# Row-major attention in spaced turns, the GELU as one operation, and weight halves made by two DMAs

## The chip, the cores and the metric

The kernel runs on one core of a Trainium2 chip. The metric is the time of one execution on the device in microseconds (us): the median of three runs is 1231.18 us (1231.11 to 1231.23). The traces were taken by the hardware profiler in one more execution each.

## The reference, cut to what matters

An encoder of two layers over 512 tokens (a grid of 8 rows of 64) with 1024 channels. All arrays are float32.

```
for l in range(2):
    h = rmsnorm(x, g_mix[l]);  z = h @ w_in[l]            # 1024 -> 2560
    q, k, v, x_rec, gate = split(z, 512 each)
    att = neighbourhood_attention(q, k, v, rel_bias[l])   # 8 heads, each token sees 8 x 16 tokens
    xc = depthwise_conv(x_rec, 4 taps)
    rec = (rg_lru forward + rg_lru backward)(xc) * gelu(gate, approximate=True)
    x = x + concat(rmsnorm(att), rmsnorm(rec)) @ w_out[l]
    h = rmsnorm(x, g_ffn[l]);  u_act, u_lin = split(h @ w_up[l])        # 1024 -> 2 x 3072
    x = x + (gelu(conv3(u_act)) * u_lin) @ w_down[l]
return rmsnorm(x, g_final)
```

The approximate GELU is `0.5 z (1 + tanh(sqrt(2/pi) (z + 0.044715 z^3)))`.

## The kernel before

Channels lie on the 128 partitions and the 512 tokens along the free axis, so an activation is some tiles of 128x512. Each float32 product is made of three matmuls in the type float32r (`mm3`, lines 187 to 190): every operand is split into a rounded half `hi` and a remainder `lo`, and `hi*hi`, `hi*lo` and `lo*hi` are summed in PSUM.

**The weights** come in chunks of 128x1024 (eight blocks of 128x128), in the order in which they are used (`weight_plan`, line 49). `load_to` (line 152) starts a DMA on SyncE's queue into one of two `raw` tiles; `split_to` (line 162) lets ScalarE copy `raw` into `hi` (line 171, which rounds) and VectorE write `raw - hi` into `lo` (line 172). There are four `hi` and four `lo` tiles, used in turn, so a chunk's halves can't be written before the chunk that stands four places ahead of it has been used. `chunk` (line 176) hands out a chunk and asks for splits three chunks ahead and loads six chunks ahead. A chunk of `w_in` is one column of the projection: 24 matmuls of 512 tokens.

**The mixing stage** of a layer begins with the four recurrent columns (`xr`), then follows the list `MIX` (line 43), a hand-written order of steps: `q`, `k`, `v`, `g` are columns of the projection (`a` and `b` its halves), `c` a convolution, `t` the gates and scans of one recurrent tile (12 matmuls and much work on ScalarE and VectorE), `u` turns a value tile into tokens by channels, `S` makes the scores and the softmax of a pair of heads for half of the columns of the grid, `T` transposes the probabilities, `P` multiplies them with the values, `o` is a part of the output projection, `n` the statistics. A planner then orders the instructions of each engine by priority and by its own costs; `urgent()` raises the priority of what stands under it, and before the change `S` and `T` stand under it as a whole (lines 724 and 727), matmuls included.

**Attention** works on tokens in column-major order (eight rows of a grid column next to each other). `query_tile` (line 509) writes two tiles per pair of heads with zeros in the other head's half (GpSimd's memsets, line 517, and four VectorE products of 64x256, line 528); `key_tile` and `value_tile` write column-major too (lines 536 and 547); line 679 turns the attention's output back to row-major. `value_tokens` lets GpSimd copy four shifted pieces into the two `edge` tiles (line 564), which `P` reads.

**The GELU of the gate** (`gate_tile`, line 573) is a VectorE evacuation (578), a square (ScalarE, 580), three VectorE operations (581, 582, 584), a Tanh (ScalarE, 583) and a last product with `fb` (585).

After the mixing stage come `w_up` and `w_down` (the MLP), whose chunks are split in the same way.

Of the kernel before, what the change touches and what calls it, by code (L numbers as in the profile page):

```python
# [99 lines left out]
def encoder(ctx: ExitStack, tc: tile.TileContext, x_d, w_d, cols_d, bias_d, out_d):  # L100
# [13 lines left out]
    p_t = pool("p_t", 12)  # L114
# [30 lines left out]
    raws, halves = {}, {}  # L145
# [5 lines left out]

    def load_to(n):
        while state["load"] < min(n, len(plan)):
            i = state["load"]
            raws[i] = p_raw.tile([P, 1024], F32, tag="raw", name=f"raw{i}")
            for n, sl in enumerate(pieces(i)):
                nc.sync.dma_start(raws[i][:, sl], w_d[i][:, sl])
                if i == n == 0:
                    nc.sync.dma_start(x[0], x_d[0])
            state["load"] += 1  # L160

    def split_to(n):
# [94 lines left out]

    NL = 16
# [168 lines left out]
    def layer(l, xn):  # L427
# [81 lines left out]
        def query_tile(i):  # L509

            qk[i] = [big(p_h, "h", f"q{l}{i}{n}") for n in range(2)]

            def zones(other):
                return [by_head(t[64 * a:64 * a + 64])[:, :, a ^ other] for t in qk[i] for a in (0, 1)]

            for z in zones(1):
                nc.gpsimd.memset(z, 0.0)  # L517
            ps = psum(ps_mm, f"qps{l}{i}")
            yield from column_parts(ps, "w_in", l, i, xg, 4)
            with urgent():  # L520
                for n, z in enumerate(zones(0)):
                    rows = slice(64 * (n % 2), 64 * (n % 2) + 64)
                    cs = slice(32 * (n // 2), 32 * (n // 2) + 32)

                    def grid(ap):
                        return by_row(ap)[rows, :, cs].rearrange("p r (j c) -> p r j c", c=8)

                    nc.vector.tensor_tensor(out=z.rearrange("p j (c r) -> p r j c", r=ROWS), in0=grid(ps),  # L528
                                            in1=grid(rb), op=ALU.mult)

        def key_tile(i):
# [10 lines left out]
        def value_tile(i):  # L542
# [3 lines left out]
            with urgent():  # L546
                nc.vector.tensor_tensor(out=by_column(o), in0=by_row(ps), in1=by_row(rb), op=ALU.mult)
# [24 lines left out]

        def gate_tile(t):
            ps = psum(ps_mm, f"gate{l}{t}")
            yield from column_parts(ps, "w_in", l, 16 + t, xg, 4)
            z = big(p_t, "t", f"z{l}{t}")
            with urgent():
                nc.vector.tensor_tensor(out=z, in0=ps, in1=rb, op=ALU.mult)
            s = big(p_t, "t", f"zs{l}{t}")
            nc.scalar.activation(s, z, AF.Square)  # L580
            nc.vector.tensor_scalar(out=s, in0=s, scalar1=0.044715, scalar2=1.0, op0=ALU.mult, op1=ALU.add)
            nc.vector.tensor_tensor(out=s, in0=s, in1=z, op=ALU.mult)
            nc.scalar.activation(s, s, AF.Tanh, scale=math.sqrt(2.0 / math.pi))
            nc.vector.scalar_tensor_tensor(out=z, in0=s, scalar=1.0, in1=z, op0=ALU.add, op1=ALU.mult)
            nc.vector.scalar_tensor_tensor(out=fb[t], in0=fb[t], scalar=0.5, in1=z, op0=ALU.mult, op1=ALU.mult)
# [17 lines left out]
        def scores(h):  # L603
            blocks = range(4 * (h % 2), 4 * (h % 2) + 4)
            bt, qt, kt = bias[h // 2], qk[h // 2][h % 2], qk[4 + h // 2]
# [4 lines left out]
            for pair in (blocks[0:2], blocks[2:4]):  # L610
                ps = psum(ps_s, f"s{l}{h}{pair[0]}")
                o = 0
                for b in pair:
                    kc0, w, _ = BLOCKS[b]
                    nc.tensor.matmul(ps[:, o:o + ROWS * w], qt[:, b % 4 * P:(b % 4 + 1) * P],  # L615
                                     kt[:, ROWS * kc0:ROWS * (kc0 + w)], start=True, stop=True)
# [3 lines left out]
                for b in pair:  # L620
                    _, w, bo = BLOCKS[b]
                    nc.vector.tensor_tensor_reduce(out=pr[b][0], in0=pr[b][1], in1=bt[:, bo:bo + ROWS * w], scale=1.0,  # L622
                                                   scalar=-3e38, op0=ALU.add, op1=ALU.max,
                                                   accum_out=mx[:, b % 4:b % 4 + 1])
                    pr[b] = pr[b][0]
            nc.vector.tensor_scalar(out=mx, in0=mx, scalar1=-1.0, scalar2=None, op0=ALU.mult)  # L626
            for b in blocks:
                nc.scalar.activation(pr[b], pr[b], AF.Exp, bias=mx[:, b % 4:b % 4 + 1],  # L628
                                     accum_out=sm[:, b % 4:b % 4 + 1])
            nc.vector.reciprocal(sm, sm)  # L630
            for b in blocks:
                nc.vector.tensor_scalar(out=pr[b], in0=pr[b], scalar1=sm[:, b % 4:b % 4 + 1], scalar2=None,
                                        op0=ALU.mult)
# [5 lines left out]
        def transposes(h, pr):  # L639
# [12 lines left out]
            for t, src, cs in ((t1, whole, slice(0, T)), (t2, part, sl)):  # L652
                nc.scalar.activation(t[0][:, cs], src[:, cs], AF.Copy)
                nc.vector.tensor_tensor(out=t[1][:, cs], in0=src[:, cs], in1=f32(t[0][:, cs]), op=ALU.subtract)
            return t1, t2

        def products(h, t1, t2):
# [45 lines left out]
        for step in MIX:  # L703
# [128 lines left out]
def lay_out(inputs):  # L832
# [33 lines left out]

    rel = a["rel_bias"]
    bias = np.full((L, H, 8, ROWS, NBIAS), MASKED, np.float32)
    for q0, (kc0, w, bo) in ((0, BLOCKS[0]), (8, BLOCKS[1]), (56, BLOCKS[7])):
        part = bias[..., bo:bo + ROWS * w].reshape(L, H, 8, ROWS, w, ROWS)  # L870
        for qr in range(ROWS):
            for c in range(8):
                qc = q0 + c
                s = min(max(qc - 8, 0), GW - 16)
                win = rel[:, :, 7 - qr:15 - qr, s - qc + 15:s - qc + 31]
                part[:, :, c, qr, s - kc0:s - kc0 + 16, :] = win.transpose(0, 1, 3, 2)
        bias[..., bo:bo + ROWS * w] = part.reshape(L, H, 8, ROWS, ROWS * w)
# [19 lines left out]
```

## Time and profile before

| | |
|---|---|
| median of three runs | 1231.18 us |
| profiled execution, whole | 1230.33 us |
| its span | 1228.5 us |
| TensorE busy | 1201.5 us (98%), 5566 matmuls |
| VectorE busy | 791.6 us (64%) |
| ScalarE busy | 488.0 us (40%) |
| GpSimd busy | 46.3 us (4%) |
| granted TensorE clock | 0.998 of 2.4 GHz |
| read from HBM | 111.06 MB, 92 GB/s |

Busy time is the union of an engine's instructions. A matmul's record is longer than the distance at which the next one follows, so a busy TensorE is not a TensorE at its peak. The stages in the trace: the first layer's `xr` columns until 28 us, its other mixing steps and output projection to 217 us, its MLP to 607 us; then the second layer's `xr` to 634 us, mixing to 822 us, MLP to 1208 us, and the last output.

### The profile page before, as it was taken

To read this page: it belongs to the slowest core of one execution; us is meant where nothing else is said; L and a number is where in the kernel's file an instruction comes from. 1 tells how busy PE (TensorE), PEld (TensorE's weight loads), DVE (VectorE), ACT (ScalarE), POOL (GpSimd) and SP (SyncE) were. 2 spreads that over 40 slices of the span, in tenths; PEclk is the share of its full clock that TensorE was granted. 3 is DMA by queue.
4 is the path that set the end of the run, shared out by engine and by line. 5 is a ranking of instruction groups with operands and counts; after the bars stand their busy time and mean duration, and the time that the engine had idled before them with its cause. 6 is when DMAs were issued, how large, how long until landed. Compare 5 with 4: busy or idle time off the path is not lost.

```text
span 1228.5 us, 14279 instructions
## 1 busy us (share of the span) xinstructions
PE 1201.5 (98%) x5566; PEld 991.2 (81%) x5566; DVE 791.6 (64%) x1257; ACT 488.0 (40%) x717; POOL 46.3 (4%) x88
## 2 busy tenths in 40 slices
PE   9999999999999999999999999999999999999997
PEld 7777778888888888888887777788888888888886
DVE  8999876865544455553659998677555255565454
ACT  6687534433221232332429765344323212223220
POOL 2001010000000000000010011100000000000000
PEclk9999999999999999999999999999999999999999
DMA  7222213223223223233222221142332322322322
GB/s 239 81 69 93 84 35 103 90 99 103 91 98 103 87 101 103 88 102 103 86 86 77 77 86 52 35 137 87 103 93 96 103 91 98 103 87 101 103 69 69
DMA packets 34355, 114.06 MB, mean 93 GB/s; under 512 B 3825, under 2 KB 7025, under 8 KB 34289
## 3 DMA queue, kind: packets, MB, share of 16 engines
q1 hardware_dynamic: 34144, 113.17, 28.1%
q8 instruction: 43, 0.70, 0.2%
q14 instruction: 24, 0.19, 0.0%
q10 hardware_dynamic: 144, 0.00, 0.0%
HBM read 111.06 MB, written 2.10 MB: 92 GB/s over the span
## 4 chain that ended last, share of the span: by engine, by line
PE 78%; DVE 11%; ACT 4%; issue 2%; DMA 1%; POOL 0%; POOLq 0%; DVEq 0%; ACTq 0%
PE dn L188 7%; PE dn L190 7%; PE dn L189 7%; PE pl L188 6%; PE pa L188 6%; PE pa L189 6%; PE pl L189 6%; PE pa L190 6%; PE pl L190 6%; PE out L188 2%; PE out L190 2%; PE out L189 2%; DVE lo L172 2%; PE up L188 1%; PE up L190 1%
## 5 line engine op out<-in xcount | busy, mean ns | idle before, releaser
L171 ACT ACTIVATE hi<-raw 128x1024 fp32r<-128x1024 f32 (+1 forms) x205 | 216.3, 1055 | 452.9 <-PE dn L189 156.6
L172 DVE TENSOR_TENSOR lo<-raw,hi 128x1024 fp32r<-128x1024 f32 (+1 forms) x205 | 249.6, 1218 | 142.9 <-ACT hi L171 142.4
L763 DVE TENSOR_TENSOR ua<-pa,g_ffn_rb 128x512 f32<-128x512 f32 x44 | 30.4, 691 | 112.9 <-PE pa L190 112.9
L771 ACT ACTIVATE uc<-uc,cols 128x512 f32<-128x512 f32 x48 | 34.8, 724 | 129.7 <-DVE uc L769 129.6
L772 DVE TENSOR_TENSOR uc<-pl,uc 128x512 f32<-128x512 f32 x44 | 30.4, 691 | 73.5 <-PE pl L190 72.0
L740 DVE TENSOR_TENSOR dns<-dn,g_ffn_rb 128x512 f32<-128x512 f32 x30 | 20.4, 689 | 29.4 <-PE dn L190 29.4
L769 DVE SCALAR_TENSOR_TENSOR uc<-ua,cols,uc 128x511 f32<-128x511 f32 x48 | 36.0, 751 | 1.5
L767 DVE SCALAR_TENSOR_TENSOR uc<-ua,cols,uc 128x511 f32<-128x511 f32 x48 | 35.8, 745 | 0.1
L628 ACT ACTIVATE prob<-prob,mx 128x192 f32<-128x192 f32 (+1 forms) x64 | 27.5, 431 | 12.0 <-DVE mx L626 11.9
L615 PEld LDWEIGHTS s<-k,q 128*128 128x128 f32 x128 | 19.6, 190 | 8.8 <-issue 4.2
L188 PE MATMUL out<-atth,hi 128*128 128x512 f32 x64 | 26.1, 407 | 0.4 <-ACT atth L684 0.4
L615 PE MATMUL s<-k,q 128*128 128x192 f32 (+1 forms) x128 | 23.2, 324 | 3.2 <-DVE mx L622 1.4
L190 PE MATMUL out<-atth,lo 128*128 128x512 f32 x64 | 25.4, 397 | 0.0
L189 PE MATMUL out<-attl,hi 128*128 128x512 f32 x64 | 25.3, 396 | 0.0
L766 DVE TENSOR_SCALAR uc<-ua,cols 128x512 f32<-128x512 f32 x48 | 23.4, 487 | 1.5
L517 POOL MEMSET q<- 64x256 f32 x32 | 10.0, 311 | 367.4 <-PE dn L189 366.1
L679 DVE COPY att<-o 64x256 f32<-64x256 f32 x32 | 19.6, 612 | 4.6 <-PE o L190 4.1
L528 DVE TENSOR_TENSOR q<-qps,g_mix_rb 64x256 f32<-64x256 f32 x32 | 20.6, 644 | 0.4
L741 DVE TENSOR_TENSOR x<-x,dns 128x512 f32<-128x512 f32 x30 | 20.1, 687 | 0.4
L622 DVE CUSTOM_DVE_ANT_0 prob<-s,bias 128x192 f32<-128x192 f32 (+1 forms) x64 | 18.2, 338 | 1.8 <-PE pte L649 0.6
L564 POOL CAST edge<-vh 64x384 fp32r<-64x384 f32 x16 | 9.4, 591 | 254.5 <-ACT vh L559 254.0
L458 DVE SCALAR_TENSOR_TENSOR xc<-xrs,cols,xc 128x511 f32<-128x511 f32 (+1 forms) x24 | 17.9, 747 | 0.4
(930 smaller groups left out, 3547.4 us busy)
## 6 DMA issues: line engine op xcount, KB each, us to landing
raw<-in_w SPq DMA_DIRECT2D x203, 512.0 KB, 3.5
x<-in_x SPq DMA_DIRECT2D x8, 256.0 KB, 5.1
out_y<-out SPq DMA_DIRECT2D x8, 256.0 KB, 2.3
bias<-in_bias SPq DMA_DIRECT2D x8, 224.0 KB, 2.5
raw<-in_w SPq DMA_DIRECT2D x2, 256.0 KB, 3.1
cols<-in_cols SPq DMA_DIRECT2D x1, 164.0 KB, 5.0
cols<-in_cols ACTq DMA_DIRECT2D x1, 4.0 KB, 3.0
```

Of the source, the lines that this page charges most:

```text
L171: nc.scalar.activation(hi[:, sl], raw[:, sl], AF.Copy)
L172: nc.vector.tensor_tensor(out=lo[:, sl], in0=raw[:, sl], in1=f32(hi[:, sl]), op=ALU.subtract)
L188: nc.tensor.matmul(ps, a[0], b[0], start=start, stop=False)
L189: nc.tensor.matmul(ps, a[0], b[1], start=False, stop=False)
L190: nc.tensor.matmul(ps, a[1], b[0], start=False, stop=stop)
L615: nc.tensor.matmul(ps[:, o:o + ROWS * w], qt[:, b % 4 * P:(b % 4 + 1) * P], kt[:, ROWS * kc0:ROWS * (kc0 + w)], start=True, stop=True)
L628: nc.scalar.activation(pr[b], pr[b], AF.Exp, bias=mx[:, b % 4:b % 4 + 1], accum_out=sm[:, b % 4:b % 4 + 1])
L763: nc.vector.tensor_tensor(out=ua, in0=pa, in1=rbf[0], op=ALU.mult)
L767: nc.vector.scalar_tensor_tensor(out=c[:, 1:], in0=ua[:, :T - 1], scalar=w[0], in1=c[:, 1:], op0=ALU.mult, op1=ALU.add)
L769: nc.vector.scalar_tensor_tensor(out=c[:, :T - 1], in0=ua[:, 1:], scalar=w[2], in1=c[:, :T - 1], op0=ALU.mult, op1=ALU.add)
L771: nc.scalar.activation(c, c, AF.Gelu_apprx_tanh, bias=col("conv_ffn_b", j, l))
L772: nc.vector.tensor_tensor(out=c, in0=pl_, in1=c, op=ALU.mult)
```

## The change

Four things change together.

1. **Weights of the mixing stage by DMA.** For the chunks of the recurrent gates and of the `q`, `k`, `v` and `g` columns (18 in each layer), `hi` is written by a DMA on GpSimd's queue that converts float32 to float32r; ScalarE writes `-hi` into `lo`; and a second DMA on GpSimd's queue adds the weights from HBM into `lo`. No `raw` tile and no VectorE subtraction is left for these. The first DMA is asked for at most three chunks ahead of use, the second at most two. The chunks of `xr`, `w_out`, `w_up` and `w_down` are made as before.
2. **Attention in row-major order.** Queries go into one constant tile `q_pair`, whose zeros are written once at the start; keys are written as they come (no reordering), and the scores' matmuls read them in runs of eight tokens; values and the output are reordered in runs of eight. The bias is laid out to match on the host. The 8 `q` tiles of the pool are gone from use.
3. **The gate's GELU** is one ScalarE operation (`Gelu_apprx_tanh`) and one product, in a step of its own (`e`).
4. **A new order `MIX`**, in which `S`, `T` and `P` of the same heads stand at least one column apart; the matmuls of `S` and `T` are no longer urgent, the VectorE and ScalarE work in them is. The pool `p_t` has 10 tiles, not 12.

```diff
-MIX = ("q0 c0 c1 k0 t0 k1 q1 c2 t1 q2 k2 c3 t2 k3 q3 S0 v0a T0 t3 v0b g0a v1a S1 u0 P0 "
-       "T1 g0b S2 v1b S3 g1a P1 u1 T2 v2a T3 P2 S4 S5 v2b g1b g2a T4 g2b P3 u2 P4 T5 S6 "
-       "v3a v3b P5 g3a T6 S7 u3 o0 g3b P6 T7 o1 P7 o2 o3 o4 n o5 o6").split()
+MIX = ("q0 c0 k0 c1 t0 S0 c2 v0 t1 c3 u0 S1 q1 T0 k1 P0 S2 t2 v1a T1 v1b P1 u1 S3 q2 T2 k2 P2 S4 t3 v2a T3 v2b "
+       "P3 u2 S5 q3 T4 k3 P4 S6 v3 T5 g0 P5 u3 S7 g1 T6 e0 e1 g2 P6 e2 g3 T7 e3 o0 o1 P7 o2 o3 o4 n o5 o6").split()
...
-    p_t = pool("p_t", 12)
+    p_t = pool("p_t", 10)
...
+    def by_dma(i):
+        w, _, bs = plan[i]
+        return w == "gate" or w == "w_in" and bs[0][1] != 12
     def load_to(n):
...
+            if by_dma(i):
+                if i > state["use"] + 3:
+                    return
+                highs[i] = p_hi.tile([P, 1024], F32R, tag="hi", name=f"hi{i}")
+                nc.gpsimd.dma_start(highs[i], w_d[i])
+                state["load"] += 1
+                continue
...
     def split_to(n):
...
+            if by_dma(i) and i > state["use"] + 2:
+                return
             load_to(i + 1)
+            if i in highs:
+                hi = highs.pop(i)
+                lo = p_lo.tile([P, 1024], F32R, tag="lo", name=f"lo{i}")
+                with urgent(0):
+                    nc.scalar.activation(lo, f32(hi), AF.Copy, scale=-1.0)
+                    nc.gpsimd.dma_start(lo, w_d[i], accum_op=ALU.add)
...
+    q_pair = const.tile([P, 8, 2, 64], F32, name="q_pair")
+    nc.gpsimd.memset(q_pair[64:P, :, 0], 0.0)
+    nc.gpsimd.memset(q_pair[0:64, :, 1], 0.0)
...
-            for z in zones(1):
-                nc.gpsimd.memset(z, 0.0)
...
+                for n in range(2):
+                    rows = slice(64 * n, 64 * n + 64)
+                    nc.vector.tensor_tensor(out=in_group(q_pair[rows, :, n]), in0=by_group(ps)[rows],
+                                            in1=by_group(rb)[rows], op=ALU.mult)
...
-                nc.vector.scalar_tensor_tensor(out=by_column(qk[4 + i]), in0=by_row(ps), scalar=0.125,
-                                               in1=by_row(rb), op0=ALU.mult, op1=ALU.mult)
+                nc.vector.scalar_tensor_tensor(out=qk[4 + i], in0=ps, scalar=0.125, in1=rb, op0=ALU.mult, op1=ALU.mult)
...
+        def gate_end(t):
+            z = branch[t]
+            nc.scalar.activation(z, z, AF.Gelu_apprx_tanh)
+            nc.vector.tensor_tensor(out=fb[t], in0=fb[t], in1=z, op=ALU.mult)
             rec_stats.add(fb[t])
...
-                    nc.tensor.matmul(ps[:, o:o + ROWS * w], qt[:, b % 4 * P:(b % 4 + 1) * P],
-                                     kt[:, ROWS * kc0:ROWS * (kc0 + w)], start=True, stop=True)
+                    nc.tensor.matmul(ps[:, o:o + ROWS * w], q_pair[:, b], kt[:, kc0 // 8:(kc0 + w) // 8],
+                                     start=True, stop=True)
...
-                with urgent():
-                    probs[n] = scores(n)
+                probs[n] = scores(n)
...
-                with urgent():
-                    turned[n] = transposes(n, probs.pop(n))
+                turned[n] = transposes(n, probs.pop(n))
```

## Rows read from the trace of the kernel before

**Rows 1.** The page: busy us of each engine (share of the span), instructions.
```profile
PE 1201.5 (98%) x5566; PEld 991.2 (81%) x5566; DVE 791.6 (64%) x1257; ACT 488.0 (40%) x717; POOL 46.3 (4%) x88
```
**Rows 2.** Windows: stretch, its length, each engine's busy us (instructions), clock, DMA.
```profile
28.00:217.00 189.00, 180.57 (x880) 145.38 (x879) 162.56 (x318) 110.84 (x198) 12.33 (x19) 1.00 0.25 80
217.00:607.00 390.00, 390.00 (x1728) 323.04 (x1727) 216.94 (x279) 122.98 (x146) 3.20 (x5) 1.00 0.29 97
634.00:822.00 188.00, 179.43 (x878) 145.14 (x877) 160.83 (x311) 112.32 (x199) 13.36 (x20) 1.00 0.23 74
...
28.00:170.00 142.00, 134.07 (x657) 107.64 (x656) 131.07 (x271) 92.96 (x172) 10.29 (x17) 1.00 0.24 77
```
**Rows 3.** Waits of PE from 28 to 217 us: us, times, longest.
```profile
PE ptw L645 <- DVE pt L654: 2.2, 3, 1.5
PE o L190 <- POOL edge L564: 1.6, 3, 1.1
PE o L188 <- DVE att L679: 1.1, 2, 0.7
PE s L615 <- DVE mx L622: 0.9, 1, 0.9
PE ptw L645 <- DVE prob L632: 0.8, 1, 0.8
PE s L615 <- DVE q L528: 0.6, 1, 0.6
PE s L615 <- DVE k L536: 0.5, 1, 0.5
```
**Rows 4.** Waits of PE from 634 to 822 us, the longest.
```profile
PE gp L188 <- DVE k L536: 1.7, 1, 1.7
...
PE ptw L645 <- DVE pt L654: 1.6, 3, 0.9
```
**Rows 5.** Groups of PE, whole run: count, busy us, mean ns.
```profile
L615 PE MATMUL s<-k,q 128*128 128x192 f32 (+1 forms) x128 | 23.2, 324 | 3.2 <-DVE mx L622 1.4 <-DVE q L528 0.9 <-DVE k L536 0.9
L188 PE MATMUL pa<-xg_g_ffn_0h,hi 128*128 128x512 f32 x44 | 17.1, 389 | 0.0
```
**Rows 6.** Groups of DVE by shape, 28 to 217 us.
```profile
L172 DVE TENSOR_TENSOR lo<-raw,hi 128x1024 fp32r<-128x1024 f32 x27 | 33.1, 1226 | 7.9 <-ACT hi L171 7.6
L528 DVE TENSOR_TENSOR q<-qps,g_mix_rb 64x256 f32<-64x256 f32 x16 | 10.3, 642 | 0.2
...
L632 DVE TENSOR_SCALAR prob<-prob,sm 128x192 f32<-128x192 f32 x24 | 6.4, 323 | 0.1
...
L536 DVE SCALAR_TENSOR_TENSOR k<-kps,g_mix_rb 128x512 f32<-128x512 f32 x4 | 4.5, 1134 | 0.0
...
L584 DVE SCALAR_TENSOR_TENSOR z<-zs,z 128x512 f32<-128x512 f32 x4 | 2.8, 688 | 1.4 <-ACT zs L583 1.4
...
L578 DVE TENSOR_TENSOR z<-gate,g_mix_rb 128x512 f32<-128x512 f32 x4 | 2.7, 679 | 0.5 <-PE gate L190 0.5
...
L581 DVE TENSOR_SCALAR zs<-zs 128x512 f32<-128x512 f32 x4 | 1.7, 422 | 0.7 <-ACT zs L580 0.7
```
**Rows 7.** Groups of ACT by shape, 28 to 217 us.
```profile
L171 ACT ACTIVATE hi<-raw 128x1024 fp32r<-128x1024 f32 x26 | 27.5, 1057 | 35.0 <-DMA raw<-in_w 7.4 <-PE qps L189 6.9 <-PE gate L189 6.2
```
**Rows 8.** DMA issues: count, KB each, median us to landing.
```profile
raw<-in_w SPq DMA_DIRECT2D x203, 512.0 KB, 3.5
x<-in_x SPq DMA_DIRECT2D x8, 256.0 KB, 5.1
```
**Rows 9.** The edge tiles' instructions, whole run: duration ns min/median/max.
```profile
L564 POOL CAST edge<-vl x16: 500/506/1314, 111.5 to 774.2; 64x384 fp32r<-64x384 f32 x16
```
**Rows 10.** Timeline at the second layer's start: start us, us, instruction.
```profile
628.56 1.91 POOL L327 TENSOR_TENSOR g_mix_r<-g_mix_ms,expo 128x4 f32<-128x4 f32 x1 [23.72 <-DVE g_mix_ms L324]
...
630.94 0.60 PE L334 MATMUL g_mix_rps<-ident,g_mix_r 128*128 128x128 f32 x4
```

More of the change, by code (lines that the diff above doesn't have):

```diff
@@ L164, in split_to @@
             i = state["split"]
+            if by_dma(i) and i > state["use"] + 2:
+                return
             load_to(i + 1)
+            if i in highs:
[4 more added lines that the diff above has]
+                    nc.gpsimd.dma_start(lo, w_d[i], accum_op=ALU.add)
+                halves[i] = (hi, lo)
+                state["split"] += 1
+                continue
             raw = raws.pop(i)
@@ L621, in scores @@
                     _, w, bo = BLOCKS[b]
-                    nc.vector.tensor_tensor_reduce(out=pr[b][0], in0=pr[b][1], in1=bt[:, bo:bo + ROWS * w], scale=1.0,
-                                                   scalar=-3e38, op0=ALU.add, op1=ALU.max,
-                                                   accum_out=mx[:, b % 4:b % 4 + 1])
+                    with urgent():
+                        nc.vector.tensor_tensor_reduce(out=pr[b][0], in0=pr[b][1], in1=bt[:, bo:bo + ROWS * w],
+                                                       scale=1.0, scalar=-3e38, op0=ALU.add, op1=ALU.max,
+                                                       accum_out=mx[:, b % 4:b % 4 + 1])
                     pr[b] = pr[b][0]
[L626 to L633, printed above, removed]
+            with urgent():
+                nc.vector.tensor_scalar(out=mx, in0=mx, scalar1=-1.0, scalar2=None, op0=ALU.mult)
+                for b in blocks:
+                    nc.scalar.activation(pr[b], pr[b], AF.Exp, bias=mx[:, b % 4:b % 4 + 1],
+                                         accum_out=sm[:, b % 4:b % 4 + 1])
+                nc.vector.reciprocal(sm, sm)
+                for b in blocks:
+                    nc.vector.tensor_scalar(out=pr[b], in0=pr[b], scalar1=sm[:, b % 4:b % 4 + 1], scalar2=None,
+                                            op0=ALU.mult)
             return st_
@@ L652, in transposes @@
             for t, src, cs in ((t1, whole, slice(0, T)), (t2, part, sl)):
-                nc.scalar.activation(t[0][:, cs], src[:, cs], AF.Copy)
-                nc.vector.tensor_tensor(out=t[1][:, cs], in0=src[:, cs], in1=f32(t[0][:, cs]), op=ALU.subtract)
+                with urgent():
+                    nc.scalar.activation(t[0][:, cs], src[:, cs], AF.Copy)
+                    nc.vector.tensor_tensor(out=t[1][:, cs], in0=src[:, cs], in1=f32(t[0][:, cs]), op=ALU.subtract)
             return t1, t2
@@ L676, in products @@
                 rows = slice(64 * a, 64 * a + 64)
-                dst = by_row(at)[rows, :, 32 * (h % 2):32 * (h % 2) + 32].rearrange("p r (j c) -> p j c r", c=8)
-                src = by_head(o)[rows, :, a].rearrange("p j (c r) -> p j c r", r=ROWS)
-                nc.vector.tensor_copy(dst, src)
+                with urgent():
+                    nc.vector.tensor_copy(by_group(at)[rows, 4 * (h % 2):4 * (h % 2) + 4],
+                                          by_head(o)[rows, :, a].rearrange("p j (r c) -> p j r c", r=ROWS))
             if h % 2:
@@ L719, in layer @@
                 convolve(n)
+            elif what == "e":
+                gate_end(n)
             elif what == "S":
@@ L867, in lay_out @@
     rel = a["rel_bias"]
-    bias = np.full((L, H, 8, ROWS, NBIAS), MASKED, np.float32)
+    bias = np.full((L, H, ROWS, 8, NBIAS), MASKED, np.float32)
     for q0, (kc0, w, bo) in ((0, BLOCKS[0]), (8, BLOCKS[1]), (56, BLOCKS[7])):
-        part = bias[..., bo:bo + ROWS * w].reshape(L, H, 8, ROWS, w, ROWS)
+        part = np.full((L, H, ROWS, 8, ROWS, w), MASKED, np.float32)
         for qr in range(ROWS):
```

43 lines of the change are left out of this document (14 added, 29 removed).

## The prediction

> **What bounds the kernel now.** I read the page's busy times first: TensorE stands at 98% [rows 1], which says that no other engine can be worth more than TensorE's gaps. The windows by stage come next, since a mean over unlike stages hides where gaps are [rows 2]. In the MLP TensorE is busy for 390.00 of 390.00 us with 1728 matmuls, one per 0.2257 us: nothing can be gained there. All gaps that matter lie in the two mixing stages, 189.00 - 180.57 = 8.43 us and 188.00 - 179.43 = 8.57 us, 17.0 in all. In the same stretches VectorE has 162.56 and 160.83 us of work, and from 28 to 170 us it is busy for 131.07 of 142 us, 92%. The waits of TensorE say what ended its gaps [rows 3, 4]: nearly always a VectorE operation (the split of the transposed probabilities, the attention's copy, the normalised probabilities, a key's evacuation) or GpSimd's edge copies, never a weight. So the stage is bound by TensorE, and what is lost beside it is latency behind a crowded VectorE queue.
>
> The gaps understate the loss. A matmul's record lasts 0.389 us [rows 5] while the next one could follow after 0.2257, so a wait is counted only from 0.163 us on. Each layer's list holds 14 waits (the ones not shown repeat these or are under 0.6 us), 28 in all: 28 x 0.163 = 4.6 us. The ceiling of any gain by removed waits is 17.0 + 4.6 = 21.6 us. The matmuls are the same in number and shape before and after, and the granted clock is already 1.00 [rows 2], so nothing more can come from TensorE itself.
>
> **The change part by part: VectorE.** Per layer:
> - 18 chunks lose the subtraction: 18 x 1.226 = 22.1 us [rows 6].
> - Queries: 16 operations of 0.642 = 10.3 us become 8 of 512 elements. Between the unreordered evacuation of the gate, 0.679, and the reordering one of the key, 1.134, I take 0.679 (runs of eight stay together): 5.4, saving 4.8; at the other end 1.2.
> - Keys are no longer reordered: 4 x (1.134 - 0.679) = 1.8. Values have the key's shape and now move in runs of eight: 1.8 by the same price, 0 at the other end. For the output copies I take no gain.
> - GELU: 0.422 and two of 0.688 go per tile: 4 x 1.80 = 7.2.
>
> The sum is 37.7 of 162.6 us (30.5 at the other ends): VectorE falls from 86% of the stretch to 66%.
>
> **ScalarE** keeps its load: the copy to `hi`, 1.057 us [rows 7], becomes the negation of the same 128x1024. What changes is what it waits for. The copy waited until a `hi` tile was free; the negation waits until the converting DMA, which starts at that same moment, has landed, and behind it in ScalarE's queue stand the exponentials, the copies of the transposes and the Tanh of the gates, for which VectorE and then TensorE wait. GELU's table has to be loaded for the MLP anyway, so its place alone moves.
>
> **Weights by DMA.** The trace has no DMA from GpSimd. A plain load of 512 KB lands after 3.5 us; at the crowded start 256 KB took 5.1 [rows 8]. The converting load I take at 3.5. The adding one reads twice the bytes: from below 3.5 us, from above twice the start's pace, 4 x 5.1 = 20.4 us; I take two plain loads in a row, 7.0, since the stage moves 80 GB/s [rows 2] and is not crowded. (The Trainium skill, "DMA: Bandwidth & Descriptors", Anatomy of one DMA, puts a GpSimd DMA at about 2.0 us plus bytes at 436 GB/s, as an estimate 3.2 us for 512 KB; the 3.5 us of SyncE's loads agree, and no run here shows one from GpSimd.) The time that there is: with four tiles in turn, a chunk's tile comes free when the chunk three ahead starts. From 28 to 170 us pass 18 chunks, one per 7.9 us, so 23.7 us on the mean against 3.5 + 1.06 + 7.0 = 11.6: covered. The tightest place is v0, behind `q0 k0 t0 S0`: 24 + 24 + 12 matmuls and a step of scores (23.2 us over 16 steps = 1.45 [rows 5]) make 60 x 0.2257 + 1.45 = 15.0 us. Also covered, by 3.4 us, which some queueing on ScalarE or GpSimd can use up: I charge 0.5 us per layer here. If the cover is gone, TensorE waits at the third matmul of the column.
>
> **GpSimd** loses 16 memsets a layer and gains 36 issues, besides its edge copies and the power for the norms. An issue that waits for a free tile holds those up. For the power, the transposes that need it start at 630.94 and it starts at 628.56 [rows 10], so an issue or two in front can push it late. An issue's own price I take as that of the nearest GpSimd row, 0.506 us [rows 9]; below it 0, above it 1.314. I charge 1.0 us per layer.
>
> **Attention and order.** Scores and transposes now stand a column or more (24 x 0.2257 = 5.4 us) behind what they read, and `P` behind `u` by two columns, where `T0` before followed `S0` after half a column. The waits of `T` (2.2 + 0.8) and of `P` (1.6 + 1.1, the same in both layers) [rows 3], 5.7 in the first layer, are of this kind and I let them go wholly; of the scores' and the key's (0.9 + 0.6 + 0.5 in the first layer, and the second's with its 1.7 [rows 4] come to 3.0) half, since `S0` still stands close behind `k0 c1 t0`. The second layer's `T` is 0.6 lower [rows 3, 4]. In sum 5.7 + 5.1 + 2.5 = 13.3 of the 16.5 us listed, and the hidden part in proportion, 4.6 x 0.8 = 3.7: 17.0 us. Against that stand 2 x (0.5 + 1.0) = 3.0, and 0.5 for the two shorter tile pools and the steps crowded at the end (`T6 e0 e1 g2`). The scores' matmuls read keys in runs of eight: nothing in the trace prices that on TensorE. At 0 from below; from above, if it cost what reordering costs VectorE (1.134 / 0.679), 23.2 x 0.67 = 15.5 us [rows 5, 6]; I take 0, because runs of eight words are nearer to the plain rows than to the single words that the key's row moves.
>
> **The sum.** 17.0 - 3.5 = 13.5 us less than the profiled execution's 1230.33 (span 1228.5, 1.8 around it) is 1216.8. The runs' median lies 0.85 above the profiled one: **1217.7, said as 1218**.
>
> **Rivals.**
> - *More goes:* with VectorE at 66% all listed waits vanish and the charges are nothing: 1231.2 - 21.6 = 1210 at best, by [rows 2]. Against it: changes between steps remain.
> - *Waits move, not vanish:* the planner places each engine's work by its own costs, and ScalarE behind its negations becomes what `T` and `P` wait for. ScalarE has 110.84 of 189 us [rows 2], so it is no bound, but it queues. A third of the gain is left: 1231.2 - 4.5 = 1227.
> - *Nothing to tell:* gains and new waits cancel, within 0.2% of 1231.2 (2.5 us, about what a measurement of this kernel can tell).
> - *The adding DMA is late (slower):* place, the third matmul of each column; it decides at v0 from 15.0 - 4.6 = 10.4 us per adding DMA and everywhere from 23.7 - 4.6 = 19.1. At 20.4, the upper bound, v0 loses 10 us and each of the other 17 about 1.3 with the queue before it: 32 a layer at most; taken at half of that, since negations are spread, 16 a layer: 1218 + 32 = 1250. For it: a read-modify-write has no row. Against it: DMA engines are 25% busy [rows 2].
> - *GpSimd's queue is late (slower):* place, the edge copies behind an issue that waits for a free tile. It decides when half a column (2.7 us), issues at 1.314 and four copies at 1.314 exceed the 11 us between `u` and `P`; then each of the four `u` steps costs about half a column: 2 x 4 x 2.7 = 21.6, 1218 + 21.6 = 1240. For it: one edge copy took 1.314 instead of 0.506 us [rows 9], so GpSimd does get held. The Trainium skill ("SBUF — State Buffer", Who interferes with whom) speaks for this one: a VectorE operation in its two-port mode holds the ports that it shares with GpSimd for the whole instruction, and DMAs issued from GpSimd starve for want of descriptors. By that rule, the single-input operations of VectorE on SBUF, the 24 of 0.323 us and their like [rows 6], would do it; the stretched copy agrees in direction, and no run here shows an issue held.
>
> **How the numbers follow.** Forecast 0.46, more 0.08, waits move 0.14, nothing 0.08, adding DMA late 0.16, GpSimd late 0.08. Faster by over 0.2%: 0.46 + 0.08 + 0.14 = 0.68; within 0.2%: 0.08; slower: 0.24. The likeliest case's own range is 1211 to 1224. For 8 in 10 the range goes up to 1242, which takes in GpSimd's case and the milder half of the DMA's, and down to 1205, below the ceiling of listed waits by the small losses that no row counts.
>
> **What would show it.** Right: from 28 to 217 us no `lo` subtraction for `w_in`; VectorE near 125 us instead of 162.6; the lists of waits without `pt`, `att` and `edge`; TensorE's gap in each mixing stage under 4 us; matmuls of the scores still 0.32 us. Wrong: TensorE's waits name a DMA into `lo`; ScalarE's longest idle stands before the negation; edge copies or the power start later than their inputs; the scores' records grow. The forecast as a whole falls if the mixing stages don't get shorter by 5 us each.

## The result and the profile after

The changed kernel takes 1240.98 us (1240.41 to 1241.66) beside 1231.20 of the kernel before: ratio 1.008 [1.0062, 1.0097], so slower, where faster was forecast. In the profiled executions the span grew by 11.0 us (1228.5 to 1239.5). The first matmul of `w_up` starts at 223.81 us in the first layer (217.84 before) and at 833.59 in the second (823.03 before): the first layer is 6.0 us longer up to there and the second adds 4.6, together 10.6 of the 11.0.

The page of the changed kernel, busy times of the engines [rows 1]:

```profile
PE 1201.8 (97%) x5566; PEld 1001.9 (81%) x5566; DVE 716.5 (58%) x1181; ACT 487.7 (39%) x713; POOL 85.4 (7%) x130
```

Its windows, with the columns of [rows 2]; the stages now end 6 and 11 us later:

```profile
28.00:223.00 195.00, 180.15 (x884) 150.79 (x883) 128.42 (x278) 112.73 (x198) 33.39 (x49) 0.97 0.52 120
...
640.00:833.00 193.00, 181.25 (x885) 151.60 (x884) 127.15 (x278) 114.88 (x199) 33.30 (x49) 0.97 0.50 119
...
50.00:75.00 25.00, 17.94 (x74) 14.48 (x74) 22.10 (x55) 24.88 (x46) 4.85 (x7) 0.83 0.66 132
150.00:200.00 50.00, 50.00 (x262) 42.35 (x261) 27.78 (x55) 24.61 (x40) 5.36 (x7) 1.00 0.28 73
```

VectorE has 34 us less to do in the first stage, as meant, and from 150 to 200 us TensorE has no gap left. But from 50 to 75 us it stands still for 7 of 25 us, and the granted clock there is 0.83, where every stretch of [rows 2] had 1.00. The groups of VectorE from 28 to 223 us show the cheaper operations [rows 6]:

```profile
L195 DVE TENSOR_TENSOR lo<-raw,hi 128x1024 fp32r<-128x1024 f32 x11 | 13.5, 1225 | 6.9 <-ACT hi L194 6.8
...
L543 DVE TENSOR_TENSOR q_pair<-qps,g_mix_rb 64x512 f32<-64x512 f32 x8 | 5.5, 689 | 2.7 <-PE qps L213 2.5
...
L551 DVE SCALAR_TENSOR_TENSOR k<-kps,g_mix_rb 128x512 f32<-128x512 f32 x4 | 2.8, 688 | 4.7 <-PE kps L213 4.7
L561 DVE TENSOR_TENSOR vt<-vps,g_mix_rb 128x512 f32<-128x512 f32 x4 | 2.7, 686 | 1.4 <-PE vps L213 1.4
```

The page's groups and DMA issues for the new way of making weights and for the scores [rows 5, 7, 8]:

```profile
L184 ACT ACTIVATE lo<-hi 128x1024 fp32r<-128x1024 f32 x36 | 38.0, 1055 | 62.2 <-DMA hi<-in_w 48.0
L164 POOL DMA_DIRECT2D hi<-in_w x36 | 23.4, 654 | 457.7 <-PE xr L213 391.6
L185 POOL DMA_DIRECT2D lo<-in_w x36 | 31.4, 874 | 133.0 <-ACT lo L184 129.7
...
L630 PE MATMUL s<-k,q_pair 128*128 128x192 f32 (+1 forms) x128 | 22.9, 323 | 0.0
...
hi<-in_w POOLq DMA_DIRECT2D x36, 512.0 KB, 4.8
lo<-in_w POOLq DMA_DIRECT2D x36, 512.0 KB, 5.6
```

ScalarE now idles 48.0 us ahead of negations because a converting load has not landed. The waits of TensorE, first layer (28 to 223 us), then second (640 to 833) [rows 3, 4]:

```profile
PE vtp L570 <- ACT a L517: 6.7, 1, 6.7
PE vps L211 <- ACT w L511: 3.6, 1, 3.6
PE vtp L570 <- DVE vt L561: 2.9, 2, 1.5
PE o L213 <- POOL edge L579: 0.7, 1, 0.7
...
PE qps L213 <- DMA lo<-in_w: 3.4, 1, 3.4
PE vps L213 <- DMA lo<-in_w: 1.8, 1, 1.8
PE kps L213 <- DMA lo<-in_w: 1.7, 1, 1.7
```

The old names `pt`, `prob`, `mx` and `att` are gone; `edge` is still there. In their place stand a few long waits: in the first layer ahead of `u` (`vtp`) and of a value column, in the second for adding DMAs, 7.6 us in all with 0.7 of a gate's (`gp`). The timeline of the changed kernel shows how the two longest of the first layer come about (GpSimd, ScalarE, VectorE, TensorE):

```profile
30.81 0.87 POOL L185 DMA_DIRECT2D lo<-in_w  x1 [5.09 <-ACT lo L184]
31.37 0.87 POOL L164 DMA_DIRECT2D hi<-in_w  x1
39.18 0.86 POOL L185 DMA_DIRECT2D lo<-in_w  x1 [6.94 <-ACT lo L184]
...
37.83 1.06 ACT L184 ACTIVATE lo<-hi 128x1024 fp32r<-128x1024 f32 x1 [4.39 <-DMA hi<-in_w]
46.25 1.06 ACT L184 ACTIVATE lo<-hi 128x1024 fp32r<-128x1024 f32 x1 [7.37 <-DMA hi<-in_w]
47.22 0.67 ACT L511 ACTIVATE w<-gp,half_b 128x512 f32<-128x512 f32 x1
...
65.89 0.68 DVE L328 TENSOR_TENSOR xcs_2l<-xc,xcs_2h 128x512 fp32r<-128x512 f32 x1
66.49 0.68 DVE L561 TENSOR_TENSOR vt<-vps,g_mix_rb 128x512 f32<-128x512 f32 x1
...
47.94 0.73 PE L211 MATMUL vps<-xg_g_mix_0h,hi 128*128 128x512 f32 x1 [3.61 <-ACT w L511]
48.46 0.63 PE L212 MATMUL vps<-xg_g_mix_0l,hi 128*128 128x512 f32 x1
48.89 0.63 PE L213 MATMUL vps<-xg_g_mix_0h,lo 128*128 128x512 f32 x1
...
67.32 1.08 PE L570 MATMUL vtp<-ident,vt 128*128 128x128 f32 x4 [6.67 <-ACT a L517]
```

First wait: a converting load stands in GpSimd's queue behind the adding DMA of the chunk before, which waits for its negation, which waits for its own converting load. So a chunk takes 46.25 - 37.83 = 8.4 us, while a column of 24 matmuls takes 5.4; and the gates' Tanh (`w`), due since about 43 us, stands in ScalarE's queue behind the negation at 46.25, so v0 starts at 47.94. I call this theory A. Second wait: v0's matmuls end near 55 us, but its urgent evacuation `vt` comes at 66.49, right behind `xcs_2l`, the low-ranking last operation of the step `c2` that is traced just ahead of `v0`; `u0`'s transposes follow 0.15 us after it. The profile names ScalarE's `a`, which ended in the same tenth of a microsecond. I call this theory D.

Both waits are paid for twice: behind each of them the matmuls start 0.43 us apart for some 3 us (from 48.46 and from 68.63 us on; granted clock 0.51 there, so 1.2 GHz), where before they follow each other after 0.2257. That is 1.4 and 1.6 us, half of what the first layer loses. In the second layer the longest wait, 3.4 us, is for the adding DMA of the third query column. It was issued at 695.10, right behind its negation, and TensorE went on at 700.92, so the transfer was not long; but ScalarE had started the negation only at 693.75, behind the exponentials of a softmax.

### The profile page after: what moved, and what is told of

It reads as the page before. It is cut to its first block, busy times and chain, and to the rows that moved or that the text cites. A ratio compares the mean times of both kernels' runs of the same rounds, so it can differ in the third digit from the quotient of the medians.

```text
span 1239.5 us, 14218 instructions
## 1 busy us (share of the span) xinstructions
PE 1201.8 (97%) x5566; PEld 1001.9 (81%) x5566; DVE 716.5 (58%) x1181; ACT 487.7 (39%) x713; POOL 85.4 (7%) x130
## 4 chain that ended last, share of the span: by engine, by line
PE 84%; issue 6%; DMA 3%; ACT 3%; DVE 2%; POOL 1%; POOLq 0%; DVEq 0%; ACTq 0%
PE pl L213 6%; PE pl L211 6%; PE pa L211 6%; PE pa L213 6%; PE pa L212 6%; PE pl L212 6%; PE dn L211 6%; PE dn L213 6%; PE dn L212 6%; DMA hi<-in_w 3%; PE out L213 2%; PE out L211 2%; PE out L212 2%; PE up L211 1%; PE gate L213 1%
## 5 line engine op out<-in xcount | busy, mean ns | idle before, releaser
L194 ACT ACTIVATE hi<-raw 128x1024 fp32r<-128x1024 f32 (+1 forms) x169 | 178.3, 1055 | 402.9 <-PE dn L212 160.8
L195 DVE TENSOR_TENSOR lo<-raw,hi 128x1024 fp32r<-128x1024 f32 (+1 forms) x169 | 205.6, 1216 | 135.3 <-ACT hi L194 135.0
L184 ACT ACTIVATE lo<-hi 128x1024 fp32r<-128x1024 f32 x36 | 38.0, 1055 | 62.2 <-DMA hi<-in_w 48.0
L164 POOL DMA_DIRECT2D hi<-in_w x36 | 23.4, 654 | 457.7 <-PE xr L213 391.6
L185 POOL DMA_DIRECT2D lo<-in_w x36 | 31.4, 874 | 133.0 <-ACT lo L184 129.7
L645 ACT ACTIVATE prob<-prob,mx 128x192 f32<-128x192 f32 (+1 forms) x64 | 27.5, 431 | 16.3 <-DVE mx L643 16.2
L638 DVE CUSTOM_DVE_ANT_0 prob<-s,bias 128x192 f32<-128x192 f32 (+1 forms) x64 | 18.5, 335 | 11.5 <-PE s L630 11.2
L696 DVE COPY att<-o 64x256 f32<-64x256 f32 x32 | 13.5, 421 | 18.6 <-PE o L213 18.4
L630 PE MATMUL s<-k,q_pair 128*128 128x192 f32 (+1 forms) x128 | 22.9, 323 | 0.0
L630 PEld LDWEIGHTS s<-k,q_pair 128*128 128x128 f32 x128 | 21.1, 198 | 0.7
```

The costliest lines, as they stand in the source:

```text
L184: nc.scalar.activation(lo, f32(hi), AF.Copy, scale=-1.0)
L185: nc.gpsimd.dma_start(lo, w_d[i], accum_op=ALU.add)
L630: nc.tensor.matmul(ps[:, o:o + ROWS * w], q_pair[:, b], kt[:, kc0 // 8:(kc0 + w) // 8], start=True, stop=True)
```

## The experiments

Times are medians beside the kernel before on the same chip (1231.0 to 1231.2), with the ratio's interval. Unless something is said, nothing is left out of the computation.

**The two parts apart.** e1 is the changed kernel with all halves made by the two engines, ScalarE and VectorE; e2 is the kernel before with the DMA weights alone.

```diff
# e1
-        return w == "gate" or w == "w_in" and bs[0][1] != 12
+        return False
# e2: before, plus by_dma and the new load_to and split_to
```

> The changed kernel with all weight halves made by ScalarE and VectorE again, as before the change; the new order, the row-major attention and the single GELU stay. Theory A (the converting load stands behind the adding DMA in GpSimd's queue, the negation on ScalarE waits for it, and the Tanh and exponentials stand behind the negation): the long gaps of TensorE between 40 and 75 us go, 1214 to 1222 us. Theory B (the adding DMA itself lands too late): the same, 1214 to 1222 us, so this run does not tell A from B. Theory C (the new order of the steps costs, whatever makes the weights): 1236 us or more, with the gaps where they are.

> The kernel before with the two DMAs for the mixing stage's weights as the only change. A: the same chain in GpSimd's queue in an order with less room between the steps, slower than before, 1238 to 1255 us, with the negation's wait for the converting load of some 40 to 60 us in sum. B: also slower, but with TensorE waiting for the adding DMA directly for over 15 us. C: faster than before, some 1225 us, because VectorE is relieved of 44 us.

e1 1239.1, [1.006, 1.0085]: without any DMA weights nearly all the loss is still there, and its longest waits are `vtp` for VectorE's `vt`, 19.0 us in four, one of 9.1. So the loss lies in what is left, and theory C, that the new list costs by itself, gave this time; the waits have theory D's pattern. e2 1246.2, [1.0095, 1.0131]: the DMA weights cost 15 us in the old list; its longest waits are `kps` for ScalarE's `w` (5.4) and the scores for `k` (4.9), and the longest that names a DMA is 1.3.

**Theory A, its queue order.** e5 lets the planner place an adding DMA only behind the next converting load. e6 gives only late columns to the DMAs.

```diff
# e5
+                if i + 1 < len(plan) and by_dma(i + 1):
+                    load_to(i + 2)
...
-                    nc.gpsimd.dma_start(lo, w_d[i], accum_op=ALU.add)
+                    with tc.issue_after(issued[i + 1].ins) if i + 1 in issued else ExitStack():
+                        nc.gpsimd.dma_start(lo, w_d[i], accum_op=ALU.add)
# e6
+        return w == "w_in" and bs[0][1] in (2, 6, 10, 3, 7, 11, 16, 17, 18, 19)
```

> The changed kernel with one edge more: on GpSimd the adding DMA of a chunk is issued behind the converting load of the next chunk. Nothing else differs. A: the load of the fifth weight column starts when its tile is free (about 34.5 us) and not at 39.7 us, the negation waits less, 1222 to 1232 us. B: the adding DMA is issued no earlier and lands no sooner, 1238 to 1243 us. C: 1238 to 1243 us.

> The changed kernel with the two DMAs only for the ten columns from the third query column on; the gates' chunks and the first six columns are split by ScalarE and VectorE. A: the early gaps go, and in the second half, where steps of attention lie between the columns, the chain has room: 1212 to 1222 us. B: TensorE still waits for adding DMAs in the second half, 1225 to 1235 us. C: 1234 us or more.

e5 1237.1, [1.0041, 1.0067]; e6 1237.4, [1.0038, 1.0064]. In e5 the holes from 25 to 50 us are gone, but the 6.7 us ahead of `u0` stand: A is worth 4 us of the 10, not the 9 or more it had promised. e6 lies in C's range: where only late columns come by DMA, the wait for `vt` stands as in e1 (16.3 us in two).

**Theory D.** One exchange in the list, in the changed kernel (e7), with weights by the engines (e8), and with e5's order (e9):

```diff
-t0 S0 c2 v0 t1 c3 u0 S1
+t0 S0 v0 c2 t1 c3 u0 S1
```

> The changed kernel with two neighbouring steps of its list exchanged: v0 ahead of c2 (S0 v0 c2 t1 c3 u0 for S0 c2 v0 t1 c3 u0). TensorE's own order up to u0 stays; on VectorE v0's evacuation then stands ahead of c2's last split instead of behind it. Theory D (the longest stall, 6.8 us ahead of u0's transposes in layer 0, and its like in layer 2, come from where v0's evacuation stands in VectorE's queue, and the 1.2 GHz stretch behind them with it): 8 to 14 us faster than the changed kernel's 1241, so 1227 to 1233, no gap over 3 us ahead of u0. Theory A (the chain load, negation, adding DMA in GpSimd's queue sets the loss): 1238 to 1242, and the gaps before v0 and at q1 stay.

> The same exchange of c2 and v0 with all weight halves made by ScalarE and VectorE as before the change (1239.1 with the new list as it is). Theory D: the stalls of 7.4 and 9.2 us ahead of u0 and the slow clock behind them go, 1220 to 1227, so faster than the kernel before by the cheaper row-major operations. If the new list costs by itself elsewhere: 1233 to 1239.

> The changed kernel with both repairs: v0 ahead of c2, and each adding DMA issued behind the next converting load (alone 1237.1). If A and D are two separate losses: 3 to 5 us under the run with the exchange alone, so 1222 to 1229. If they are the same idle time seen twice: within 1 us of the better of the two.

e7 1226.9, [0.9954, 0.998]: 14 us from two exchanged steps. e8 1231.9, [0.9996, 1.0014], 7 us and less than D gave; e9 1222.2, [0.9908, 0.9936], 4.7 under e7, so in this list A and D are two losses. The timeline of e7 (VectorE, then TensorE) shows `vt` 8 us ahead of `xcs_2l` and `u0` behind v0 without a hole:

```profile
55.68 0.68 DVE L561 TENSOR_TENSOR vt<-vps,g_mix_rb 128x512 f32<-128x512 f32 x1
64.14 0.67 DVE L328 TENSOR_TENSOR xcs_2l<-xc,xcs_2h 128x512 fp32r<-128x512 f32 x1
...
57.69 0.60 PE L570 MATMUL vtp<-ident,vt 128*128 128x128 f32 x4
```

In e8 the same thing has moved on to the next such pair. Its timeline (ScalarE, TensorE): `u0`'s transposes are done near 53 us, yet their copy `vh` comes at 74.59, behind `c3`'s `xcs_3h`, and P0 waits for it:

```profile
73.11 0.63 ACT L327 ACTIVATE xcs_3h<-xc 128x512 fp32r<-128x512 f32 x1 [2.57 <-DVE xc L486]
...
74.59 0.58 ACT L574 ACTIVATE vh<-vtp 128x512 fp32r<-128x512 f32 x1
...
75.22 0.58 PE L211 MATMUL o<-pt,vh 128*128 128x256 f32 x1 [3.60 <-ACT vh L574]
```

So e16 (from e8) and e17 (from e9) exchange that pair too:

```diff
-t0 S0 v0 c2 t1 c3 u0 S1
+t0 S0 v0 c2 t1 u0 c3 S1
```

> The new list with weight halves by the two engines, v0 ahead of c2 (alone 1231.9) and also u0 ahead of c3. Theory D (an urgent copy stands in its engine's queue behind the low-ranking one of the step traced just ahead of it, here v0's vh behind c3's split on ScalarE): the holes of 3.8 us (layer 0) and 7.2 us (layer 2) ahead of P0's matmuls go with the 1.2 GHz stretches behind them: 1214 to 1224. If the new list is slow for its dense early half (scores, scans and gates at once) and the holes only show where: 1229 to 1232.

> The same second exchange in the changed kernel with v0 ahead of c2 and each adding DMA behind the next converting load (1222.2). There VectorE is freer and no hole stands ahead of P0: theory D gives 1218 to 1222; if u0's earlier copies push the gates back on ScalarE: 1222 to 1227.

e16 1218.4, [0.9886, 0.9913]: 13.5 us more. e17 1222.1, [0.9919, 0.9944]: nothing; e9's trace has no wait for `vh` that could go. The timeline of e16 has the two copies the other way round:

```profile
64.24 0.58 ACT L574 ACTIVATE vh<-vtp 128x512 fp32r<-128x512 f32 x1
78.07 0.63 ACT L327 ACTIVATE xcs_3h<-xc 128x512 fp32r<-128x512 f32 x1 [1.80 <-DVE xc L486]
```

**The cheaper operations alone.** e10 is e1 with the old list (`e0` to `e3` put in behind their gates). The old list makes all queries ahead of the first scores, so the one shared `q_pair` loses three of four pairs: in e10 their scores read the last pair's queries, and what they should be is left out. e11 keeps a pair of query tiles per pair of heads and twelve tiles in `p_t`, as before. e15 is the kernel before with the GELU alone.

```diff
# e11
+            qk[i] = [big(p_h, "h", f"q{l}{i}{m}").rearrange("p (b n c) -> p b n c", b=4, n=2) for m in range(2)]
+            for q in qk[i]:
+                nc.gpsimd.memset(q[64:P, :, 0], 0.0)
+                nc.gpsimd.memset(q[0:64, :, 1], 0.0)
# e15: the four lines from "s = big(...)" and the two products with 1.0 and 0.5 become
+            nc.scalar.activation(z, z, AF.Gelu_apprx_tanh)
+            nc.vector.tensor_tensor(out=fb[t], in0=fb[t], in1=z, op=ALU.mult)
```

> Row-major attention and the one-operation GELU in the old list of steps, weight halves by the two engines: the cheaper operations alone. Theory D with the new list as the loss: the waits for pt, att and edge shrink with VectorE's 22 us less per layer, 1222 to 1229. If the old list's gaps are set by ScalarE and by the list, and not by VectorE's busy time: 1229 to 1233. Slower than 1233 if the row-major views cost more than the trace shows.

> Row-major attention and the one-operation GELU in the old list, weight halves by the two engines, with the query tiles kept per pair of heads as before the change (two evacuations more per pair), since the old list makes all queries ahead of the first scores and one shared tile loses them there. If the 1214.3 of the run with one shared tile is the price of the operations in the old list: 1213 to 1217. If it was an effect of the shared tile (no waits on it, no zeroing): 1222 or more.

> The kernel before with nothing but the GELU as one operation: four operations less on VectorE and one less on ScalarE per gate tile, all in the late half of a mixing stage. From the waits of the kernel before, few of which lie there: 1228 to 1231. If the gate's chain holds the sum of squares at the stage's end: 1224 to 1228. If the new function costs ScalarE table switches: 1232 or more.

e10 1214.3, [0.9847, 0.9875]; e11 1210.8, [0.9826, 0.9851]: both faster than any of the ranges. Row-major attention and the GELU are worth 20 us in the old list, together with the changed priorities, which e10 and e11 keep (the matmuls of `S` and `T` not urgent, and also the output copies of `P` urgent, which the list of changes doesn't name); no run tells these apart. e1 and e10 differ in the list alone, so the new list costs 1239.1 - 1214.3 = 24.8 us. e15 1225.6, [0.9946, 0.9972]: the GELU alone gives 5.4, more than I had expected of it; in its trace the waits for `att` fall from 2.3 to 0.4 us, and those for `prob` (1.5) are gone.

**The DMA weights in the old list.** e12 is e11 with the change's DMA functions, e13 with e5's order, e14 with e6's columns.

> The whole change but for its list: row-major, GELU and the converting and adding DMAs in the old list of steps. If the DMA weights cost in the old list what they cost there beside the old operations (1246.2 against 1231.1): 1226 to 1231. If VectorE's 39 us less per layer pay for their lateness: 1213 to 1220. If the list is all that is wrong with the change, and the DMAs relieve VectorE as meant: under 1213.

> The run before with each adding DMA issued behind the next converting load. Theory A (the serial chain in GpSimd's queue is what the DMA weights cost): 4 to 12 us under the run before it, 1212 to 1222. If the cost is the transfers' own length, or ScalarE's negations ahead of its other work: within 2 us of the run before it.

> The whole change in the old list with only ten of the twenty-eight chunks of a mixing stage by DMA (query, key and value columns 2 and 3 and the gate projections). If each DMA chunk costs alike: about 10/18 of 19.1 us stay, 1220 to 1223. If the cost lies in the first columns, whose loads have least lead: 1211 to 1215. If it lies in the late ones: 1226 to 1231.

e12 1229.9, [0.9989, 1.0007]; e13 1231.4, [0.9996, 1.0019]; e14 1224.6, [0.9936, 0.9963]. The DMA weights cost 19 us over e11, 13.8 with ten chunks of eighteen (more than their share), and the order of issue alone gives nothing back: A as I had put it falls here. In e13's trace the holes are elsewhere: the value columns wait 7.2 us for adding DMAs, which e12's did not. e18 put the negation on GpSimd:

```diff
-                    nc.scalar.activation(lo, f32(hi), AF.Copy, scale=-1.0)
+                    nc.gpsimd.tensor_scalar(out=lo, in0=f32(hi), scalar1=-1.0, scalar2=None, op0=ALU.mult)
```

> The whole change in the old list (1229.9, of which the DMA weights are 19.1) with the negation on GpSimd in place of ScalarE. If the DMA weights cost by ScalarE's queue (a negation that waits for the converting load holds the gates and exponentials behind it): 4 to 15 us faster, 1215 to 1226, and the wait of kps for ScalarE's w goes. If they cost because the halves land late whoever negates: 1230 or more, GpSimd's own operation being longer than the 1.06 us on ScalarE.

1305.9, [1.0598, 1.0632]: GpSimd takes 2.912 us on the mean for what ScalarE does in 1.06, so the run tells nothing of ScalarE's queue. Left was the lead. Before, a load went into one of two `raw` tiles up to six chunks ahead; a converting load needs its `hi` tile and may be three ahead. e20 (from e12) and e21 (from e13) buy a fifth `hi` tile:

```diff
-    p_t = pool("p_t", 12)
+    p_t = pool("p_t", 10)
-    p_hi = pool("p_hi", 4)
+    p_hi = pool("p_hi", 5)
-                if i > state["use"] + 3:
+                if i > state["use"] + 4:
-            if by_dma(i) and i > state["use"] + 2:
+            if by_dma(i) and i > state["use"] + 3:
```

> The whole change in the old list (1229.9) with a fifth tile for upper halves (paid with two of the twelve general tiles), so that the converting loads and the negations stand one chunk further ahead of their use. If the DMA weights cost by too little lead (a load, a negation and an adding DMA in a row of 4.7, 1.06 and 5.9 us, begun when a tile comes free): 1214 to 1224. If lead isn't the cause, or the two tiles are missed elsewhere: 1228 or more.

> The same fifth tile with each adding DMA behind the next converting load (without the tile 1231.4). If lead is the cause and the two repairs add: 1211 to 1220. If the further loads collide with the adding DMAs in the queue or on the 16 engines: 1225 or more.

e20 1210.9, [0.9823, 0.985]; e21 1210.4, [0.9819, 0.9846]: the whole 19 us are gone, so the lead is what the DMA weights lacked. The edit gives more lead in two ways, a tile more for the converting loads and negations and adding DMAs that are asked for one chunk earlier, and no run tells the two apart; nor was e11 run with a fifth tile. The timeline of e12 (GpSimd, ScalarE, TensorE) has A's ring. In e21's (GpSimd, ScalarE), which has e13's order too, a load is issued ahead of the adding DMA that waits, negations come 3.8 and 4.8 us apart, and `w` starts 5.3 us earlier:

```profile
30.93 0.85 POOL L186 DMA_DIRECT2D lo<-in_w  x1 [4.70 <-ACT lo L185]
31.49 0.85 POOL L165 DMA_DIRECT2D hi<-in_w  x1
39.03 0.85 POOL L186 DMA_DIRECT2D lo<-in_w  x1 [6.69 <-ACT lo L185]
...
45.84 1.06 ACT L185 ACTIVATE lo<-hi 128x1024 fp32r<-128x1024 f32 x1 [6.59 <-issue]
46.81 0.67 ACT L509 ACTIVATE w<-gp,half_b 128x512 f32<-128x512 f32 x1
...
47.53 0.79 PE L212 MATMUL kps<-xg_g_mix_0h,hi 128*128 128x512 f32 x1 [4.64 <-ACT w L509]
```

```profile
29.18 0.56 POOL L165 DMA_DIRECT2D hi<-in_w  x1 [3.27 <-PE xr L217]
33.29 0.86 POOL L189 DMA_DIRECT2D lo<-in_w  x1 [3.54 <-ACT lo L187]
...
31.93 1.06 ACT L187 ACTIVATE lo<-hi 128x1024 fp32r<-128x1024 f32 x1 [4.95 <-DMA hi<-in_w]
...
35.70 1.06 ACT L187 ACTIVATE lo<-hi 128x1024 fp32r<-128x1024 f32 x1 [2.18 <-DMA hi<-in_w]
...
40.52 1.06 ACT L187 ACTIVATE lo<-hi 128x1024 fp32r<-128x1024 f32 x1 [1.36 <-PE gp L216]
41.48 0.67 ACT L512 ACTIVATE w<-gp,half_b 128x512 f32<-128x512 f32 x1
```

The windows of e12, then of e21, say the same in two rows each: TensorE's busy time (first) and clock (third from the end) from 28 to 50 us, and VectorE's busy time (third) over the stage. The last row is e20's: with the tile but in e12's order of issue part of the early hole stays, and the time is the same.

```profile
28.00:50.00 22.00, 17.36 (x72) 13.98 (x71) 11.36 (x20) 7.43 (x11) 4.25 (x6) 0.89 0.66 152
...
28.00:217.00 189.00, 178.55 (x878) 148.43 (x877) 127.81 (x285) 114.41 (x199) 37.00 (x61) 0.98 0.50 123
```

```profile
28.00:50.00 22.00, 22.00 (x98) 18.21 (x97) 14.38 (x25) 12.66 (x17) 5.93 (x10) 1.00 0.87 200
...
28.00:217.00 189.00, 186.99 (x930) 156.87 (x929) 138.63 (x300) 122.54 (x210) 36.15 (x59) 1.00 0.53 129
```

```profile
28.00:50.00 22.00, 20.09 (x82) 16.13 (x81) 12.63 (x21) 9.52 (x14) 4.36 (x6) 0.92 0.86 200
```

All together, medians in us (the old list's column with e11's query tiles):

| row-major and GELU, with | old list | new list | v0 before c2 | and u0 before c3 |
|---|---|---|---|---|
| weights by the engines | 1210.8 | 1239.1 | 1231.9 | 1218.4 |
| DMA weights, four `hi` | 1229.9 | 1241.0 | 1226.9 | not run |
| the same, next load first | 1231.4 | 1237.1 | 1222.2 | 1222.1 |
| DMA weights, five `hi` | 1210.9 | not run | not run | not run |
| five `hi`, next load first | 1210.4 | not run | not run | not run |

The versions with 1210 beat both kernels, the one before by 1.6 to 1.7% and the changed one by 2.4 to 2.5%. Which of the three is best can't be told.

## Why the prediction was wrong, by its steps

The parts add up: the cheaper operations give 16.7 us in e10, the new list takes 24.8 and the DMA weights take 1.9, together 10.0 more, and 9.8 were measured. That the time lies inside the range for 8 in 10 (1205 to 1242) is luck: its upper end stood there for late edge copies and a long adding DMA, and neither is the cause.

- **The bound and the ceiling** held: TensorE bounds, and 20.3 (e11) and 20.7 (e21) of the 21.6 us were there. That "nothing more can come from TensorE itself" was true of gains only: after long waits its clock fell, which I had put at nothing.
- **VectorE** held: forecast were 37.7 us less per layer, and the page has 791.6 - 716.5 = 75.1 in two layers (123.5 us from 28 to 217 us, forecast 125; the changed kernel is 6 us behind there). The other ends add up to 32.3 a layer, not to 30.5. Queries at 0.689, keys at 0.688 and values at 0.686 us came as taken (0.679); the output copies cost 0.421 instead of 0.612, for which I had charged no gain.
- **ScalarE's** load held (488.0 and 487.7 us). That the GELU's table load only changes its place did not: function tables are loaded 24 times instead of 20, at 1.28 us each. No run shows what that costs.
- **Strided scores at nothing** held: 323 ns beside 324.
- **Attention and order, 17.0 us: failed, and with the largest error.** "The waits of `T` ... and of `P` ... I let them go wholly" is true by name of `pt`, `prob` and `att`, not of `edge` (0.7 and 1.4 us left). But it was not the new order's distance that took them away: in e11's trace, in the old list with the changed priorities, these waits for VectorE are gone too. And I took the list as a change of distances only, and did not ask which low-ranking operation each urgent one now stands behind. The new list costs 24.8 us (e1 beside e10); two exchanges of neighbours give back 7.2 and 13.5. The 4.1 that are left, and the 3.5 between e10 and e11 (query tiles, `p_t`), stay unexplained. The pattern stood in the change itself, `c2 v0` and `c3 u0`: a convolution, which waits for VectorE and ScalarE in turn, just ahead of a step that TensorE needs. It is not enough by itself: the old list has `c1 k0`, and no wait for a key there is over 1.7 us [rows 3, 4].
- **Weights by DMA, "covered, by 3.4 us ... I charge 0.5 us per layer": failed.** The chain came out as taken, 4.8 + 1.06 + 5.6 = 11.5 us by medians against 11.6 (3.5 + 1.06 + 7.0), but by luck: the converting load was 1.3 us too short and the adding one 1.4 too long. (The Trainium skill's "DMA: Bandwidth & Descriptors", Anatomy of one DMA, gave 3.2 us as an estimate for a DMA of 512 KB from GpSimd; the converting loads measured 4.8, so the measurement decides.) What failed was the cover. I set the chain against one chunk per 7.9 us, a mean over the stage, and against matmuls alone, where columns follow each other after 5.4 us at the start, and I let the chains of neighbouring chunks overlap, which they do not in these queues of GpSimd and ScalarE: the ring has a period of 8.4 us. Its price was 19 us in the old list; with a fifth tile and a chunk more of lead it is nothing, with the adding transfer no shorter (median 6.5 us in e21, 5.9 in e12). In the new list it showed as only 1.9 us, because list and DMAs idle the same stretch: after the exchange of v0 and c2 the version with DMA weights is even 5 us faster than the one without.
- **GpSimd**: the issues cost 0.654 and 0.874 us, between the bounds (none over 0.93). The power for the second layer was late: ready at 634.39 us, it stood behind one adding DMA until 636.60, and TensorE waited 0.9 us for it.
- **Rivals.** "Waits move" named the right place, ScalarE behind its negations, and priced it as a gain kept by a third; that it could turn the sign I did not see. "The adding DMA is late" is found by name in the second layer, 7.6 us at the third matmul of four columns, where it was to be. Its mechanism, the transfer's length, is not the cause: the transfers took 5.3 to 8.5 us, below the 10.4 from which it was to decide; the one traced above was late because its negation was, and with more lead (e20, e21) these waits are gone. "GpSimd's queue is late" by edge copies didn't come (2.0 us of `edge` waits instead of 3.2); what was late in that queue were converting loads.

Not settled: why the planner puts an urgent copy behind the low-ranking one of the step ahead; where the new list's last 4.1 us and the 3.5 between e10 and e11 lie; how the 20 us of e11 divide; which half of the fifth tile's edit gives the lead; and whether a fifth tile in the repaired new list would go below 1210.

## What to carry to other kernels

A buffer that is filled by one engine and then rewritten by another counts as lead: when a staging tile goes, count how many chunks ahead the first transfer can start, and set the whole chain, with the queues that tie one chunk's chain to the next, against the shortest spacing of its uses, not the mean. When an order of steps changes, read for each step that TensorE needs what stands directly ahead of its first copy on VectorE and ScalarE, and what that waits for. Two changes that stall the same stretch hide each other, so each has to be tried in the order of steps where the other is absent.

## What was not expected of the hardware

- A converting load of 512 KB from GpSimd lands after 4.8 us in the changed kernel (median; 4.0 to 6.2 over the runs), a plain one from SyncE after 3.4 to 3.5; an adding one after 5.6 (5.5 to 7.0). The issue keeps GpSimd busy for 0.654 and 0.874 us.
- GpSimd needs 2.912 us to negate 128x1024 float32 (mean of e18), ScalarE 1.055.
- After the 3.6 us stall ahead of v0, the granted clock fell to 0.51: matmuls start 0.43 us apart from 48.46 to 51.45 us and 0.23 apart after it, so this stall is paid for a second time at 1.2 GHz.
